# A causal convolution of matrices on one core: one-bank seeds, weights cast while they are loaded, and a start on TensorE

## The chip, the cores and the metric

One core of a Trainium2 chip runs the whole program. The time is the device time of one execution in microseconds (us). The span of a profile is about 2 us shorter than the time, which also holds the launch. TensorE does the matmuls, VectorE and ScalarE the elementwise work, GpSimd issues the DMAs that cast, and SyncE the plain ones and the DMA transposes.

## The reference

```python
B, S, D, K = 8, 4096, 512, 8
out = np.zeros_like(x)                       # x: (B, S, D) fp32, kernel: (K, D, D) fp32
for k in range(K):
    shifted = x if k == 0 else np.concatenate(
        [np.zeros((B, k, D), dtype=np.float32), x[:, :-k, :]], axis=1)
    out += np.matmul(shifted, kernel[k])
```

Each output row is a sum of eight row-by-matrix products. The kernel cuts the 32,768 rows into 128 runs of 256 time steps, one run a partition, and takes eight time steps of all runs at once: this is "a step" below, and there are 32. Applying a three-products-for-four scheme three times over, it does 27 products a step instead of 64. The price is sums: of weights once, of x in each step, and of partial results.

## The kernel before

A step has three nodes (MID, LO, HI) of nine products. A product is four matmuls of 128 x 128 x 512. A node begins with a "seed": a shared partial sum in two banks of PSUM (512 fp32 a bank), from which its two outputs start.

```python
    def node_u(i, a):
        ...
        product(n.q[:, 1], n.s[0], W[a, MID, MID], True)
        nc.scalar.copy(out=n.q[:, 0], in_=n.q[:, 1])          # between banks
    def node_a(n):
        product(n.q[:, 0], n.s[1][0], W[n.a, MID, LO], False)
        product(n.q[:, 1], n.s[1][1], W[n.a, MID, HI], False)
        nc.scalar.copy(out=n.ts, in_=n.q)                     # two banks to SBUF
    def node_v(n, b_):
        product(p[:, 1], n.s[2][b_], W[n.a, b_, MID], True)
        tt(p, p[:, 1:2].to_broadcast([P, 2, D]), n.ts, ADD if b_ == LO else SUB)   # VectorE, two banks
```

Within the node loop the sums of x stand between the nodes' work. D421's upper half, which the HI node multiplies, is summed after the seeds of that node:

```python
        if nxt:
            node_v(nxt, 0)
            node_v(nxt, 1)
        ...
        elif a == LO:
            prep_d421(HI)
```

At the start, x goes through DMA transposes. Then the weights come in four rounds of fp32, each summed in fp32 by VectorE and cast or negated by ScalarE:

```python
        for c in range(DC):                      # 4 rounds, all 27 weights need all 4
            ... nc.sync.dma_start(out=wt, in_=kr[:, c, 4 * h:4 * h + 4, :])
            ... tt(mid4, ...); tt(mid2, ...); tt(W[a, b_, MID][:, c], V[:, 0], V[:, 1], ADD)
            ... nc.scalar.copy(...); nc.scalar.mul(..., mul=-1.0)
```

## Time and profile before

| | kernel before |
|---|---|
| time, median of 3 | 925.17 us (924.97 to 925.95) |
| span of the profiled run | 922.9 us |
| TensorE's first full stretch of matmuls | at 112.21 us, 1 of 864 products done |
| one step | 25.165 us |
| TensorE's own work in a step | 108 x 0.216 = 23.33 us |
| VectorE busy in a step | 23.22 us |
| waits in the even stage | 59.9 us |

The last row: the last matmul ends at 917.71, so the even stage takes 917.71 - 112.21 = 805.5 us. The 863 products left take 863 x 4 x 0.216 = 745.6 us. The rest, 59.9 us, is time in which TensorE waits. Two parts of the time can therefore be cut: the start, and the step's wait. The views that show this stand in the prediction.

### The profile page before, as it was taken

How to read it: one execution, taken by the hardware profiler on the slowest of the kernel's cores; microseconds unless marked ns; L12 is line 12 of the kernel's file. 1: busy time of each engine (PE TensorE's matmuls, PEld its weight loads, DVE VectorE, ACT ScalarE, POOL GpSimd, SP SyncE). 2: the span in 40 equal slices, each digit the busy share in tenths (PEclk: the TensorE clock that was granted, in tenths of full speed). 3: DMA queues.
4: the chain of work that ended last, by engine and by line, in shares of the span. 5: the costliest groups of instructions: out<-in, count | busy, mean ns of one | idle time of the engine just before them, and what ended most of it. 6: DMA issues, size and time to landing. Idle time of an engine off the chain costs nothing.

```text
span 922.9 us, 9305 instructions
## 1 busy us (share of the span) xinstructions
PE 758.2 (82%) x3464; PEld 336.7 (36%) x3464; DVE 793.2 (86%) x954; ACT 255.9 (28%) x329; POOL 43.0 (5%) x86
## 2 busy tenths in 40 slices
PE   1000199999999999999999999999999999999997
PEld 0000044444444444444444444444444444444443
DVE  0358679999999999999999999999999999999996
ACT  0046622222222222222222222222222222222222
POOL 4000000000000000000000000000000000000000
PEclk9999999999999999999999999999999999999999
DMA  7853317867787767677776676767677876676642
GB/s 95 116 202 130 91 40 165 181 153 174 178 173 172 158 163 179 153 161 165 182 173 157 173 180 166 155 166 177 143 172 165 181 167 166 171 182 165 155 136 114
DMA packets 169709, 145.25 MB, mean 157 GB/s; under 512 B 140752, under 2 KB 140752, under 8 KB 169664
## 3 DMA queue, kind: packets, MB, share of 16 engines
q1 hardware_dynamic: 159936, 110.12, 44.0%
q0 software_dynamic: 9728, 34.54, 23.7%
q8 instruction: 27, 0.44, 0.2%
q14 instruction: 18, 0.15, 0.1%
HBM read 77.46 MB, written 67.11 MB: 157 GB/s over the span
## 4 chain that ended last, share of the span: by engine, by line
PE 61%; DVE 21%; issue 5%; ACT 0%; DVEq 0%
PE pp L181 61%; DVE D L79 11%; DVE pp L79 7%; DVE y L79 4%; ACT ts L209 0%; DVEq L79 0%; ACT w L172 0%; ACT pp L202 0%
## 5 line engine op out<-in xcount | busy, mean ns | idle before, releaser
L181 PE MATMUL pp<-w,D 128*128 128x512 bf16 x3328 | 730.5, 380 | 61.9 <-DVE D L79 53.2
L181 PEld LDWEIGHTS <-D 128*128 128x128 bf16 x3328 | 323.2, 98 | 479.0 <-DVE D L79 69.0
L79 DVE TENSOR_TENSOR pp<-pp,ts 128x1024 f32<-128x1024 f32 x192 | 226.5, 1225 | 26.2 <-ACT ts L209 26.2
L79 DVE TENSOR_TENSOR D<-D 128x512 bf16<-128x512 bf16 (+3 forms) x353 | 239.5, 731 | 0.0
L79 DVE TENSOR_TENSOR y<-pp,ms 128x1024 f32<-128x1024 f32 x128 | 156.3, 1221 | 46.4 <-PE pp L181 46.4
L79 DVE TENSOR_TENSOR D<-XT 128x512 bf16<-128x512 bf16 (+3 forms) x226 | 152.5, 722 | 34.0 <-DMA XT<-xin 34.0
L209 ACT COPY ts<-pp 128x1024 f32<-128x1024 f32 x96 | 97.2, 1013 | 276.3 <-PE pp L181 272.8
L202 ACT COPY pp<-pp 128x512 f32<-128x512 f32 x96 | 54.7, 570 | 236.4 <-PE pp L181 236.4
L181 PE MATMUL pp<-w,XT 128*128 128x512 bf16 x128 | 34.2, 385 | 96.2 <-DVE w L79 96.2
L226 ACT COPY ms<-pp 128x1024 f32<-128x1024 f32 x64 | 64.9, 1014 | 69.5 <-PE pp L181 69.5
L91 POOL DMA_DIRECT2D xin<-in_x_dram x64 | 34.0, 531 | 827.9 <-DMA XT<-xin 827.9
L181 PEld LDWEIGHTS <-XT 128*128 128x128 bf16 x128 | 12.5, 98 | 98.5 <-issue 83.8
L79 DVE TENSOR_TENSOR mid<-wt 128x1024 f32<-128x1024 f32 (+1 forms) x12 | 18.9, 1576 | 17.2 <-DMA wt<-in_kernel_dram 17.2
L171 ACT CAST w<-mid 128x512 bf16<-128x512 f32 x20 | 12.1, 605 | 71.8 <-DVE mid L79 71.8
L79 DVE TENSOR_TENSOR w<-mid 128x512 bf16<-128x512 f32 x20 | 13.1, 689 | 0.4
L172 ACT ACTIVATE w<-mid 128x512 bf16<-128x512 f32 x20 | 12.5, 625 | 0.0
L79 DVE TENSOR_TENSOR w<-wt 128x512 bf16<-128x512 f32 x16 | 10.3, 684 | 0.0
L172 ACT ACTIVATE w<-wt 128x512 bf16<-128x512 f32 x16 | 10.0, 625 | 0.0
L171 ACT CAST w<-wt 128x512 bf16<-128x512 f32 x16 | 9.6, 602 | 0.0
L95 POOL DMA_DIRECT2D xin<-in_x_dram x16 | 8.3, 530 | 1.2 <-DVE xin L93 1.2
L79 DVE TENSOR_TENSOR mid<-mid 128x1024 f32<-128x1024 f32 x4 | 4.9, 1225 | 0.3
L85 PE MATMUL pp<-zero,ident 128*128 128x512 bf16 x8 | 3.6, 630 | 1.4 <-POOL ident masks.py:199 1.4
(10 smaller groups left out, 5.3 us busy)
## 6 DMA issues: line engine op xcount, KB each, us to landing
out_dram<-y SPq DMA_DIRECT2D x128, 512.0 KB, 3.0
xin<-in_x_dram POOLq DMA_DIRECT2D x64, 512.0 KB, 5.4
wt<-in_kernel_dram SPq DMA_DIRECT2D x8, 1024.0 KB, 4.8
XT<-xin SPq DMA_TRANSPOSE x66, 5.0
xin<-in_x_dram POOLq DMA_DIRECT2D x16, 60.0 KB, 2.6
```

The lines of the kernel that those rows point to most:

```text
L79: nc.vector.tensor_tensor(out=o, in0=a, in1=b, op=op)
L85: nc.tensor.matmul(pw[:, h], lhsT=ident, rhs=zero, start=True, stop=True)
L91: nc.gpsimd.dma_start(out=xin, in_=xr[:, K * i + 4 * h:K * i + 4 * h + 4, :])
L95: nc.gpsimd.dma_start(out=xin[b * G + 1:(b + 1) * G], in_=xr[b * G:(b + 1) * G - 1, RUN - 8 + 4 * h:RUN - 4 + 4 * h, :])
L171: nc.scalar.copy(out=W[a, b_, LO][:, c], in_=V[:, 1])
L172: nc.scalar.mul(out=W[a, b_, HI][:, c], in_=V[:, 0], mul=-1.0)
L181: nc.tensor.matmul(bank, lhsT=comp[:, c * P:(c + 1) * P], rhs=w[:, c, :], start=start and c == 0, stop=c == DC - 1, skip_group_check=True)
L202: nc.scalar.copy(out=n.q[:, 0], in_=n.q[:, 1])
L209: nc.scalar.copy(out=n.ts, in_=n.q)
L226: nc.scalar.copy(out=ms[b_], in_=p)
```

## The change

Its intent is to halve VectorE's work on seeds, to put D421 ahead of them, and to begin multiplying as soon as the first weights are there. The core of the diff:

```diff
+    def node_a1(i, a):
+        product(n.q[:, 1], n.s[1][1], W[a, MID, HI], True)
         nc.scalar.copy(out=n.q[:, 0], in_=n.q[:, 1])
+    def node_a0u(n):
         product(n.q[:, 0], n.s[1][0], W[n.a, MID, LO], False)
-        product(n.q[:, 1], n.s[1][1], W[n.a, MID, HI], False)
-        n.ts = cpool.tile([P, 2, D], f32, name="ts")
-        nc.scalar.copy(out=n.ts, in_=n.q)
+        product(n.q[:, 1], n.s[0], W[n.a, MID, MID], False)
+    def node_seed(n):                            # ScalarE puts the seed into one bank of each pair
+        for b_ in range(2):
+            n.p[b_] = ppool.tile([P, 2, D], f32, name="pp")
+            ... nc.scalar.copy / nc.scalar.mul(-1.0) (out=n.p[b_][:, 1], in_=n.q[:, 1])
+        nc.scalar.copy(out=n.dts, in_=n.q[:, 0])
     def node_v(n, b_):
-        product(p[:, 1], n.s[2][b_], W[n.a, b_, MID], True)
-        tt(p, p[:, 1:2].to_broadcast([P, 2, D]), n.ts, ADD if b_ == LO else SUB)
+        product(p[:, 1], n.s[2][b_], W[n.a, b_, MID], False)
+        ... tt(p[:, 0], n.dts, p[:, 1], SUB)     # VectorE: one bank (or scalar_tensor_tensor)
... sums of x merged, with row steps of -7, -3, -6:
-        tt(D1[:, 0], XT[:, 7], XT[:, 0], SUB)
-        tt(D1[:, 1], XT[:, 0], XT[:, 1], SUB)
+        tt(D1[:, 0:2], XT[:, 7::-7], XT[:, 0:2], ADD)
... the start: each tap one DMA that casts fp32 to bf16; mids summed as bf16
+    def load_w(tap):
+        n = K - 1 - tap
+        nc.gpsimd.dma_start(out=W[n >> 2, n >> 1 & 1, n & 1], in_=kr[:, :, tap, :])
+    for tap in (6, 4, 7, 5): load_w(tap)         # weights of the LO node first
+    xi.append(load_x(0, 1))
+    for tap in (2, 0, 3, 1): load_w(tap)
+        transpose_pe(T, xi[0], range(0, 4))      # TensorE transposes the first step's x
+        transpose_pe(H, D421, range(0, 8))       # and the rows before it
... order of nodes and of TensorE's products
-    order = [(i, a) for i in range(NIT) for a in (MID, LO, HI)]
+    order = [(0, LO), (0, HI), (0, MID)]
+    order += [(i, a) for i in range(1, NIT) for a in (MID, LO, HI)]
         if nxt:
-            node_a(nxt)
+            node_a0u(nxt)
+        if k >= 2:
+            node_l(cur, 1, LO)                   # one product between the seed and its use
+        ... node_seed(nxt); ... prep_d421(HI); ... node_v(nxt, 0); node_v(nxt, 1)
```

More of the change, by code (lines that the diff above doesn't have):

```diff
@@ L53 @@
     xpool = ctx.enter_context(tc.tile_pool(name="x", bufs=2))
-    ppool = ctx.enter_context(tc.tile_pool(name="p", bufs=4, space=PSUM))
     ctx.enter_context(tc.manual_schedule())
@@ L63 @@
     W = {}
-    for a in (MID, LO, HI):
-        for b_ in (MID, LO, HI):
-            for c_ in (MID, LO, HI):
+    for a in (LO, HI, MID):
+        for b_ in (LO, HI, MID):
+            for c_ in (LO, HI, MID):
                 W[a, b_, c_] = wpool.tile([P, DC, D], bf, name=f"w{a}{b_}{c_}")
@@ L76 @@
     D1 = spool.tile([P, 2, D], bf, name="D1")
+    F2 = spool.tile([P, 5, D], bf, name="F2")
+    F21 = spool.tile([P, 4, D], bf, name="F21")
+    F1 = spool.tile([P, 2, D], bf, name="F1")
+    F0 = spool.tile([P, D], bf, name="F0")
     def tt(o, a, b, op):
         nc.vector.tensor_tensor(out=o, in0=a, in1=b, op=op)
-    for _ in range(4):
-        pw = ppool.tile([P, 2, D], f32, name="pp")
-        for h in range(2):
-            nc.tensor.matmul(pw[:, h], lhsT=ident, rhs=zero, start=True, stop=True)
     def load_x(i, h):
         xin = xpool.tile([P, 4, D], bf, name="xin")
-        if i >= 0:
-            nc.gpsimd.dma_start(out=xin, in_=xr[:, K * i + 4 * h:K * i + 4 * h + 4, :])
-        else:
-            nc.vector.memset(xin, 0.0)
-            for b in range(B):
-                nc.gpsimd.dma_start(
-                    out=xin[b * G + 1:(b + 1) * G],
-                    in_=xr[b * G:(b + 1) * G - 1, RUN - 8 + 4 * h:RUN - 4 + 4 * h, :])
+        nc.gpsimd.dma_start(out=xin, in_=xr[:, K * i + 4 * h:K * i + 4 * h + 4, :])
         return xin
@@ L103, in transpose_x, with pairs @@
             in_=xin.rearrange("p j d -> p (j d)"))
+    def pairs(z):
+        return z.rearrange("p (a b) d -> p a (b d)", b=2)
     def prep_m():
-        tt(D1[:, 0], XT[:, 7], XT[:, 0], SUB)
-        tt(D1[:, 1], XT[:, 0], XT[:, 1], SUB)
-        tt(D2[:, 0:2], XT[:, 6:8], XT[:, 0:2], ADD)
-        tt(D2[:, 2:4], XT[:, 0:2], XT[:, 2:4], ADD)
+        tt(D1[:, 0:2], XT[:, 7::-7], XT[:, 0:2], ADD)
+        tt(pairs(D2[:, 1:5]), pairs(XT)[:, 3::-3], pairs(XT)[:, 0:2], ADD)
     def prep_d27():
-        tt(D2[:, 4], XT[:, 5], XT[:, 7], ADD)
+        tt(D2[:, 0], XT[:, 5], XT[:, 7], ADD)
     def prep_d21():
-        tt(D21[:, 0], D2[:, 4], D2[:, 0], SUB)
-        tt(D21[:, 1:4], D2[:, 0:3], D2[:, 1:4], SUB)
+        tt(D21[:, 0:4], D2[:, 0:4], D2[:, 1:5], ADD)
     def prep_d4(h):
@@ L121, in prep_d4, with prep_d41, prep_d42 @@
         tt(D4[:, 4 * h:4 * h + 4], a, b, ADD)
-    def prep_d41_d42(h):
+    def prep_d41(h):
         if h == LO:
-            tt(D41[:, 0], D4[:, 7], D4[:, 0], SUB)
-            tt(D41[:, 1], D4[:, 0], D4[:, 1], SUB)
-            tt(D42[:, 0:2], D4[:, 6:8], D4[:, 0:2], ADD)
-            tt(D42[:, 2:4], D4[:, 0:2], D4[:, 2:4], ADD)
-        else:
-            tt(D41[:, 2:4], D4[:, 3:5], D4[:, 4:6], SUB)
+            tt(D41[:, 0:2], D4[:, 7::-7], D4[:, 0:2], ADD)
+        else:
+            tt(D41[:, 2:4], D4[:, 3:5], D4[:, 4:6], ADD)
+    def prep_d42(h):
+        if h == LO:
+            tt(pairs(D42)[:, 0:2], pairs(D4)[:, 3::-3], pairs(D4)[:, 0:2], ADD)
+        else:
             tt(D42[:, 4:8], D4[:, 2:6], D4[:, 4:8], ADD)
@@ L134, in prep_d421 @@
         if h == LO:
-            tt(D421[:, 0], D42[:, 7], D42[:, 0], SUB)
-            tt(D421[:, 1:4], D42[:, 0:3], D42[:, 1:4], SUB)
-        else:
-            tt(D421[:, 4:8], D42[:, 3:7], D42[:, 4:8], SUB)
-    xi = [load_x(-1, 0), load_x(-1, 1)]
-    for h in range(2):
-        transpose_x(xi[h], h)
-    tt(D4[:, 5:8], XT[:, 1:4], XT[:, 5:8], ADD)
-    tt(D42[:, 7], D4[:, 5], D4[:, 7], ADD)
-    tt(D2[:, 4], XT[:, 5], XT[:, 7], ADD)
-    xi = [load_x(0, 0), load_x(0, 1)]
-    transpose_x(xi[0], 0)
@@ L149 @@
-    prep_m()
-    prep_d4(LO)
-    prep_d21()
-    prep_d41_d42(LO)
-    transpose_x(xi[1], 1)
-    prep_d4(HI)
-    xi = [load_x(1, 0), load_x(1, 1)]
-    with tc.tile_pool(name="wt", bufs=1) as tp:
-        for c in range(DC):
-            halves = []
-            for h in range(2):
-                wt = tp.tile([P, 4, D], f32, name="wt", bufs=3)
-                nc.sync.dma_start(out=wt, in_=kr[:, c, 4 * h:4 * h + 4, :])
-                halves.append(wt)
-            mid4 = tp.tile([P, 4, D], f32, name="mid4")
-            tt(mid4, halves[0], halves[1], SUB)
-            for a, A in ((MID, mid4), (LO, halves[1]), (HI, halves[0])):
-                mid2 = tp.tile([P, 2, D], f32, name="mid2", bufs=2)
-                tt(mid2, A[:, 0:2], A[:, 2:4], SUB)
-                for b_, V in ((MID, mid2), (LO, A[:, 2:4]), (HI, A[:, 0:2])):
-                    tt(W[a, b_, MID][:, c], V[:, 0], V[:, 1], ADD)
-                    nc.scalar.copy(out=W[a, b_, LO][:, c], in_=V[:, 1])
-                    nc.scalar.mul(out=W[a, b_, HI][:, c], in_=V[:, 0], mul=-1.0)
@@ L174 @@
-    mpool = ctx.enter_context(tc.tile_pool(name="m", bufs=3))
+            tt(D421[:, 0:4:2], D42[:, 7:0:-6], D42[:, 0:4:2], ADD)
+            tt(D421[:, 1:4:2], D42[:, 0:4:2], D42[:, 1:4:2], ADD)
+        else:
+            tt(D421[:, 4:8], D42[:, 3:7], D42[:, 4:8], ADD)
+    nc.vector.memset(D421, 0.0)
+    xi = [load_x(0, 0)]
+    for b in range(B):
+        nc.gpsimd.dma_start(out=D421[b * G + 1:(b + 1) * G, 1:8],
+                            in_=xr[b * G:(b + 1) * G - 1, RUN - 7:RUN, :])
+    def load_w(tap):
+        n = K - 1 - tap
+        nc.gpsimd.dma_start(out=W[n >> 2, n >> 1 & 1, n & 1], in_=kr[:, :, tap, :])
@@ new lines, in mid_a, with mid_b, mid_c, transpose_pe @@
+    def mid_a(b_, c_):
+        tt(W[MID, b_, c_], W[HI, b_, c_], W[LO, b_, c_], SUB)
+    def mid_b(a, c_):
+        tt(W[a, MID, c_], W[a, HI, c_], W[a, LO, c_], SUB)
+    def mid_c(a, b_):
+        tt(W[a, b_, MID], W[a, b_, LO], W[a, b_, HI], SUB)
+    for tap in (6, 4, 7, 5):
+        load_w(tap)
+    xi.append(load_x(0, 1))
+    for tap in (2, 0, 3, 1):
+        load_w(tap)
+    with tc.tile_pool(name="t", bufs=1, space=PSUM) as tpool:
+        H = tpool.tile([P, K, D], bf, name="hist")
+        T = tpool.tile([P, K, D], bf, name="xt0")
+        def transpose_pe(o, src, ts_):
+            for t in ts_:
+                for c in range(DC):
+                    nc.tensor.transpose(o[:, t, c * P:(c + 1) * P],
+                                        src[:, t % src.shape[1], c * P:(c + 1) * P], ident)
+        transpose_pe(T, xi[0], range(0, 4))
+        transpose_pe(H, D421, range(0, 8))
+        nc.scalar.copy(out=XT[:, 0:4], in_=T[:, 0:4])
+        nc.scalar.copy(out=F0, in_=T[:, 0])
+        hs = D421[:, 4:8]
+        nc.scalar.copy(out=hs, in_=H[:, 4:8])
+        tt(D4[:, 5:8], H[:, 1:4], hs[:, 1:4], ADD)
+        tt(D4[:, 0:4], hs, XT[:, 0:4], ADD)
+        prep_d41(LO)
+        mid_b(LO, HI)
+        tt(D42[:, 7], D4[:, 5], D4[:, 7], ADD)
+        prep_d42(LO)
+        mid_c(LO, LO)
+        prep_d421(LO)
+        mid_b(LO, LO)
+        mid_c(LO, MID)
+        mid_c(LO, HI)
+        transpose_pe(T, xi[1], range(4, 8))
+        nc.scalar.copy(out=XT[:, 4:8], in_=T[:, 4:8])
+        tt(F1[:, 0], hs[:, 3], XT[:, 0], ADD)
+        tt(F1[:, 1], XT[:, 0], XT[:, 1], ADD)
+        tt(F2[:, 0], hs[:, 1], hs[:, 3], ADD)
+        tt(F2[:, 1:3], hs[:, 2:4], XT[:, 0:2], ADD)
+        tt(F2[:, 3:5], XT[:, 0:2], XT[:, 2:4], ADD)
+        tt(F21, F2[:, 0:4], F2[:, 1:5], ADD)
+        prep_d4(HI)
+        prep_d41(HI)
+        prep_d42(HI)
+        prep_d421(HI)
+        prep_d27()
@@ L175 @@
+    xi = [load_x(1, 0), load_x(1, 1)]
+    ppool = ctx.enter_context(tc.tile_pool(name="p", bufs=3, space=PSUM))
+    qpool = ctx.enter_context(tc.tile_pool(name="q", bufs=1, space=PSUM))
+    for k in range(4):
+        pw = ppool.tile([P, 2, D], f32, name="pp") if k else qpool.tile([P, 2, D], f32, name="qq")
+        for h in range(2):
+            nc.tensor.matmul(pw[:, h], lhsT=ident, rhs=zero, start=True, stop=True)
+    mpool = ctx.enter_context(tc.tile_pool(name="m", bufs=2))
     cpool = ctx.enter_context(tc.tile_pool(name="c", bufs=2))
@@ L186, with streams @@
         pass
-    def streams(a):
+    def streams(i, a):
+        if a == MID and i == 0:
+            return (F0, [F1[:, 0], F1[:, 1]], [F2[:, 1], F2[:, 3]],
+                    [F21[:, j] for j in range(4)])
         if a == MID:
-            return (XT[:, 0], [D1[:, 0], D1[:, 1]], [D2[:, 0], D2[:, 2]],
+            return (XT[:, 0], [D1[:, 0], D1[:, 1]], [D2[:, 1], D2[:, 3]],
                     [D21[:, j] for j in range(4)])
@@ L195, in streams @@
                 [D421[:, o + j] for j in range(4)])
-    def node_u(i, a):
+    def node_a1(i, a):
         n = Node()
-        n.i, n.a, n.s = i, a, streams(a)
-        n.q = ppool.tile([P, 2, D], f32, name="pp")
-        product(n.q[:, 1], n.s[0], W[a, MID, MID], True)
+        n.i, n.a, n.s = i, a, streams(i, a)
+        n.q = qpool.tile([P, 2, D], f32, name="qq")
+        product(n.q[:, 1], n.s[1][1], W[a, MID, HI], True)
         nc.scalar.copy(out=n.q[:, 0], in_=n.q[:, 1])
+        n.p = {}
         return n
-    def node_a(n):
+    def node_a0u(n):
         product(n.q[:, 0], n.s[1][0], W[n.a, MID, LO], False)
-        product(n.q[:, 1], n.s[1][1], W[n.a, MID, HI], False)
-        n.ts = cpool.tile([P, 2, D], f32, name="ts")
-        nc.scalar.copy(out=n.ts, in_=n.q)
-        n.p = {}
-    def node_v(n, b_):
-        n.p[b_] = p = ppool.tile([P, 2, D], f32, name="pp")
-        product(p[:, 1], n.s[2][b_], W[n.a, b_, MID], True)
-        tt(p, p[:, 1:2].to_broadcast([P, 2, D]), n.ts, ADD if b_ == LO else SUB)
+        product(n.q[:, 1], n.s[0], W[n.a, MID, MID], False)
+    def node_seed(n):
+        for b_ in range(2):
+            n.p[b_] = ppool.tile([P, 2, D], f32, name="pp")
+            if b_ == LO:
+                nc.scalar.copy(out=n.p[b_][:, 1], in_=n.q[:, 1])
+            else:
+                nc.scalar.mul(out=n.p[b_][:, 1], in_=n.q[:, 1], mul=-1.0)
+        n.dts = cpool.tile([P, D], f32, name="dts")
+        nc.scalar.copy(out=n.dts, in_=n.q[:, 0])
+    def node_v(n, b_):
+        p = n.p[b_]
+        product(p[:, 1], n.s[2][b_], W[n.a, b_, MID], False)
+        if b_ == LO:
+            tt(p[:, 0], n.dts, p[:, 1], SUB)
+        else:
+            nc.vector.scalar_tensor_tensor(out=p[:, 0], in0=p[:, 1], scalar=-1.0,
+                                           in1=n.dts, op0=MUL, op1=SUB)
     ms = {}
@@ L220, in node_l, with store @@
         product(n.p[b_][:, j], n.s[3][2 * b_ + j], W[n.a, b_, j], False)
+    def store(i, a, b_, y):
+        t0 = K * i + 4 * a + 2 * b_
+        nc.sync.dma_start(out=orr[:, t0:t0 + 2, :], in_=y)
+    first = {}
     def node_e(n, b_):
         p = n.p[b_]
-        if n.a == MID:
+        if n.i == 0 and n.a == MID:
+            for a in (LO, HI):
+                y = first[a, b_]
+                tt(y, y, p, ADD if a == LO else SUB)
+                store(0, a, b_, y)
+        elif n.a == MID:
             ms[b_] = mpool.tile([P, 2, D], f32, name="ms")
@@ L228, in node_e @@
             y = ypool.tile([P, 2, D], f32, name="y")
-            tt(y, p, ms[b_], ADD if n.a == LO else SUB)
-            t0 = K * n.i + 4 * n.a + 2 * b_
-            nc.sync.dma_start(out=orr[:, t0:t0 + 2, :], in_=y)
-    order = [(i, a) for i in range(NIT) for a in (MID, LO, HI)]
-    nodes = [node_u(*order[0])]
-    node_a(nodes[0])
+            if n.i == 0:
+                nc.scalar.copy(out=y, in_=p)
+                first[n.a, b_] = y
+            else:
+                tt(y, p, ms[b_], ADD if n.a == LO else SUB)
+                store(n.i, n.a, b_, y)
+    order = [(0, LO), (0, HI), (0, MID)]
+    order += [(i, a) for i in range(1, NIT) for a in (MID, LO, HI)]
+    nodes = [node_a1(*order[0])]
+    node_a0u(nodes[0])
+    node_seed(nodes[0])
     node_v(nodes[0], 0)
     node_v(nodes[0], 1)
-    nodes.append(node_u(*order[1]))
     for k, (i, a) in enumerate(order):
         cur = nodes[k]
-        nxt = nodes[k + 1] if k + 1 < len(order) else None
-        last = i + 1 == NIT
-        if a == MID and not last:
+        stage = k % 3
+        more = i + 1 < NIT
+        if stage == 0 and more:
             transpose_x(xi[0], 0)
@@ L246 @@
         node_l(cur, 0, HI)
-        node_e(cur, 0)
-        if nxt:
-            node_a(nxt)
-        if a == MID:
-            prep_d421(LO)
-        elif not last and a == LO:
-            prep_m()
-            prep_d4(LO)
-        elif not last:
+        if k < 2:
+            node_l(cur, 1, LO)
+            node_l(cur, 1, HI)
+            node_e(cur, 0)
+            if k == 0:
+                mid_b(HI, HI)
+                mid_c(HI, LO)
+                mid_b(HI, LO)
+                mid_c(HI, MID)
+                mid_c(HI, HI)
+                nodes.append(node_a1(*order[1]))
+            else:
+                mid_a(LO, HI)
+                mid_a(HI, HI)
+                mid_b(MID, HI)
+                mid_a(LO, LO)
+                mid_a(HI, LO)
+                mid_b(MID, LO)
+                mid_c(MID, MID)
+                mid_c(MID, LO)
+                mid_c(MID, HI)
+                nodes.append(node_a1(*order[2]))
+            node_e(cur, 1)
+        nxt = nodes[k + 1] if k + 1 < len(order) else None
+        if nxt:
+            node_a0u(nxt)
+        if k >= 2:
+            node_l(cur, 1, LO)
+            node_e(cur, 0)
+        if nxt:
+            node_seed(nxt)
+        if stage == 0:
+            if i:
+                prep_d421(LO)
+                prep_d41(HI)
+        elif stage == 1:
+            if more:
+                prep_m()
+            if i:
+                prep_d421(HI)
+        elif more:
+            prep_d41(LO)
+            prep_d42(LO)
             prep_d21()
-            prep_d41_d42(LO)
         if nxt:
@@ L260 @@
             node_v(nxt, 1)
-        if a == MID:
-            prep_d41_d42(HI)
-            prep_d27()
-        elif a == LO:
-            prep_d421(HI)
-        elif not last:
-            prep_d4(HI)
-        node_l(cur, 1, LO)
-        if k + 2 < len(order):
-            nodes.append(node_u(*order[k + 2]))
-        node_l(cur, 1, HI)
-        node_e(cur, 1)
-        if a == LO and not last:
+        if stage == 0:
+            if i:
+                prep_d42(HI)
+                prep_d27()
+        elif more:
+            prep_d4(LO if stage == 1 else HI)
+        if k >= 2:
+            node_l(cur, 1, HI)
+        if 1 <= k and k + 2 < len(order):
+            nodes.append(node_a1(*order[k + 2]))
+        if k >= 2:
+            node_e(cur, 1)
+        if stage == 1 and more:
             transpose_x(xi[1], 1)
```

## The prediction

> **What bounds the kernel now.** I read the page first, for the shares, then the windows of the start and of three single steps, then the waits, then the timeline of one step, and last the groups by form for the price of each kind of instruction.
>
> ```profile
> span 922.9 us, 9305 instructions
> PE 758.2 (82%) x3464; PEld 336.7 (36%) x3464; DVE 793.2 (86%) x954; ACT 255.9 (28%) x329; POOL 43.0 (5%) x86
> PE   1000199999999999999999999999999999999997
> PEclk9999999999999999999999999999999999999999
> ```
>
> The shares name no winner: VectorE 86%, TensorE 82%. But the slices show two kernels: a start in which TensorE does nothing, then one even stage at full clock. So I take them apart.
>
> ```profile
> 0.00:112.00 112.00, 5.93 (x12) 1.49 (x13) 57.11 (x70) 39.47 (x74) 11.74 (x27) 1.00 0.59 129
> 311.53:336.69 25.16, 23.48 (x108) 10.50 (x109) 23.22 (x29) 6.78 (x8) 1.06 (x2) 1.00 0.70 167
> 336.69:361.86 25.17, 23.49 (x109) 10.51 (x109) 23.22 (x29) 6.78 (x8) 1.06 (x2) 1.00 0.73 168
> 361.86:387.02 25.16, 23.48 (x108) 10.46 (x109) 23.22 (x29) 6.78 (x8) 1.06 (x2) 1.00 0.71 167
> ```
>
> The columns are PE, PEld, DVE, ACT, POOL busy with instruction counts, then clock and DMA. A step (8 time steps of every run, 27 products of 4 matmuls) takes 25.165 us, 32 of them. Neither engine fills it. What is missing is one wait:
>
> ```profile
> PE pp L181 <- DVE w L79: 96.2, 4, 53.6
> PE pp L181 <- DVE D L79: 53.2, 32, 1.7
> ```
>
> The first line is the start (TensorE waits for combined weights), the second is once a step: 53.2 / 32 = 1.66 us. The timeline shows which instruction ends it:
>
> ```profile
> 311.53 21.76 PE L181 MATMUL pp<-w,D 128*128 128x512 bf16 x100 [1.68 <-DVE D L79]
> 330.15 3.09 DVE L79 TENSOR_TENSOR D<-XT 128x512 bf16<-128x512 bf16 x5
> 333.12 1.03 PE L181 MATMUL pp<-w,XT 128*128 128x512 bf16 x4
> 333.15 2.36 DVE L79 TENSOR_TENSOR pp<-pp,ts 128x1024 f32<-128x1024 f32 x2
> 334.24 0.57 ACT L202 COPY pp<-pp 128x512 f32<-128x512 f32 x1 [2.49 <-PE pp L181]
> 335.42 1.22 DVE L79 TENSOR_TENSOR D<-D 128x2048 bf16<-128x2048 bf16 x1
> ```
>
> VectorE makes five sums of x, then the two seeds of a node (1.2 us each), and only then D421's upper half (ends 336.64), which TensorE's next product needs; it resumes at 336.69. VectorE is late, in order, on a step in which it is busy 23.2 us. TensorE's own floor: 100 matmuls in 21.76 us, the last one lasting 0.38, so (21.76 - 0.38) / 99 = 0.2160, and over 80 in 17.45 (chain of waits) 0.2161; I use 0.216. 108 x 0.216 = 23.33 us. So a step holds 25.165 - 23.33 = 1.84 us that is not matmul: the 1.68 us wait plus the 0.16 us by which the last matmul before it outlasts its pitch.
>
> **What the Trainium skill says.** "TensorE: Matmul & The Clock Gate", section "Wait - 56ns, not 53.3ns?", gives 215.7 ns from start to start of warm 512-column matmuls and 426.7 cold. The trace agrees: 0.216 in the step, and about 0.43 for the first matmuls after an idle start (weight loads at 112.59, 113.02, 113.44). So 23.3 us is a floor for a step.
>
> "VectorE: DVE Perf Modes", section "The perf-mode tier table", has tensor_tensor run two elements a cycle for bf16 in SBUF and one for any PSUM operand. The trace agrees:
>
> ```profile
> L79 DVE TENSOR_TENSOR pp<-pp,ts 128x1024 f32<-128x1024 f32 x139 | 164.0, 1225 | 11.7 <-ACT ts L209 11.7
> L79 DVE TENSOR_TENSOR y<-pp,ms 128x1024 f32<-128x1024 f32 x92 | 112.3, 1221 | 33.0 <-PE pp L181 33.0
> L79 DVE TENSOR_TENSOR D<-D 128x2048 bf16<-128x2048 bf16 x46 | 55.9, 1216 | 0.0
> L79 DVE TENSOR_TENSOR D<-D 128x1024 bf16<-128x1024 bf16 x69 | 45.3, 683 | 0.0
> L79 DVE TENSOR_TENSOR D<-D 128x512 bf16<-128x512 bf16 x92 | 36.4, 416 | 0.0
> ```
>
> 1024 fp32 from PSUM cost as much as 2048 bf16. "Vector Engine (DVE) Microarchitecture Reference", section 5.1, lists operands with a negative step among what is not measured; the change uses them, and no run here shows them yet. "DMA: Bandwidth & Descriptors", section "SWDGE vs HWDGE vs iDMA", ties a cast during DMA to the GpSimd queue. The x loads of before are such casts, so their rate is a measured stand-in for the weights.
>
> **The change, part by part.** (1) One-bank seeds. Before, a node's VectorE work is two 1024-wide fp32 sums; after, ScalarE copies the seed into one bank of each pair and VectorE makes only the other: two of 512. The y rows have 1221 for 1024; by the skill's one element a cycle (0.96 GHz) half as many save 0.53, so 0.69 us. Six a step: 7.35 falls to 4.14.
> (2) The bf16 sums of a step merge from 18 instructions to 13: seven of 2048, five of 1024, one of 512: 7 x 1.216 + 5 x 0.684 + 0.417 = 12.35 us. Before: 4 x 1.216 + 5 x 0.684 + 2 x 0.951 + 7 x 0.417 = 13.1.
> (3) y stays, 4 x 1.221 = 4.88. VectorE's sum is 12.35 + 4.14 + 4.88 = 21.4 against 25.3. Consecutive instructions overlap by about 0.08 (a 2048 sum started at 310.26, the next at 311.39: 1.13 for 1.21); before, 25.3 shows as 23.2 busy. After: some 19.8 to 20.1.
> (4) ScalarE: per node the copy between banks, two seeds and one fp32 half, 4 x 0.57 = 2.28, plus two ms copies a step: 3 x 2.28 + 2 x 1.01 = 8.9 us, from 6.8. Far from a bound.
> (5) Order: D421's upper half now goes ahead of the node's seed sums. I laid one node (9 products, 7.78 us) on a time line. In the two heavy nodes VectorE starts y at 1.97 us (product 2 ends 1.73, plus 0.16 tail, plus 0.09 to the start), does y and three sums by 6.0, the seed halves by 7.3, D4 by 8.4, y by 9.5, i.e. 1.8 us into the next node, just in time; in the light node it rests 2 us. TensorE needs the first seed half at 7.78 and has it at 6.7. So the 1.84 us go.
> (6) A new round trip comes: the product after the seeds needs ScalarE's copy. From the trace the copy starts 0.09 us after the end of the product (333.12 + 1.03 = 334.15, copy at 334.24), lasts 0.57, and TensorE resumes 0.06 after (112.15 to 112.21). The last matmul of the seed product starts at s and ends at s + 0.38, so the seed is there at s + 1.10. The change puts one other product in between, so the slot is s + 5 x 0.216 = s + 1.08. A stall of 0.02 to 0.03 a node: 95 nodes, 2.4 us in all.
>
> **The start.** Before, the first full stretch of matmuls begins at 112.21, and only one product of the 864 is done by then.
>
> ```profile
> 68.96 2.29 DVE L79 TENSOR_TENSOR mid<-wt 128x2048 f32<-128x2048 f32 x1 [3.19 <-DMA wt<-in_kernel_dram]
> 111.58 0.57 ACT L202 COPY pp<-pp 128x512 f32<-128x512 f32 x1
> 112.21 19.77 PE L181 MATMUL pp<-w,D 128*128 128x512 bf16 x84 [8.67 <-ACT pp L202]
> q0 software_dynamic: 9728, 34.54, 23.7%
> ```
>
> The weights come in four rounds of 14.8 us (54.16, 68.96, ...) after 43.6 us of DMA transposes. After, everything comes on the GpSimd queue as bf16. Its rate by the last line: 34.54 MB / (0.237 x 922.9 us) = 158 GB/s. Up to the second half of x lie 0.52 + 0.86 + 4 x 0.52 + 0.52 = 4.0 MB: 25 us, plus 4 for first issue and landing: 29 to 30. TensorE, in order, may not pass its transposes: 16 x 0.11 = 2, the ScalarE copy of 2048 (1.9, from 0.57 for 512 and 1.01 for 1024), 8 warm-up matmuls at 0.43 = 3.4: the first node starts near 37.5. A node alone is 9 x 0.864 plus 0.9 for each of its two ScalarE trips and some 0.2: 9.75. First node to 47.2, second to 57 (its last weight lands near 43, so it doesn't wait). The third needs nine sums of weights on VectorE, which start after the second node's seeds, about 54.2: nine at 1.13 plus self-waits, 64.8; then two sums of x, 66.5, its first seed half, 67.2. There the steady stage starts, with 23 products done and 841 left: 841 x 0.864 = 726.6. Sum: 67 + 727 + 2.4 + tail 5.2 (last matmul ended at 917.7 of 922.9) + 2.3 (925.17 less the span) = 804; I take a us off for sums that overlap: 803 us. Against 925 the saving splits into some 58 us of steps (1.84 x 31.5) and some 65 of the start (112 to 67, and 22 products at 0.864 more done by then), less the new trips.
>
> **The rivals.** Negative row steps lose the two-a-cycle rate: five of the merged sums slow down, three of 1024 by 0.53 and two of 2048 by 1.07: 3.7 us a step, VectorE at 23.8, above TensorE's 23.3, with waits a step of 24.3 and a total near 834. For: the skill calls it unmeasured. Against: inside a row all is dense, with step 1. Second, the seed trip is longer than one product: each 0.1 us more per node costs 9.5 us, 812. Against: the latencies above are of the same copy in the same place. Third, the starting loads are slower, as their rows are shorter (1 KB written a packet, 4 KB for x) and eight are of 15 partitions: at 110 GB/s the first node starts 11 us later, 814; at 180, 3 us earlier. Fourth, the DMA transpose of x now starts later in its step: it lands 5.5 us after issue (313.07 to the buffer's release at 318.61), near 7.7 us of the node in which VectorE wants it at 7.2. The light node after it absorbs this; if not, 0.5 us a step, 818.
>
> **Range and chances.** The rivals of the start move the time by -4 to +11, those of the step by 0 to +30, of which I hold 0 to +10 likely. So 790 to 822 eight times in ten. Even with the worst two together it stays under 850, 8% less; faster by over 2% 0.98, within 2% 0.015, slower 0.005.
>
> **What would show it.** Steps of 23.3 to 23.5 us, the wait for D gone, VectorE busy about 20 of them, seed halves at 0.69, merged sums at 1.22 and 0.68; TensorE waiting on ScalarE under 5 us in the steady stage; the steady stage from about 67 us. It would be wrong with steps over 24 us, or with the steady stage starting past 80 us.

## The result, and the profile after

The changed kernel takes **795.83 us** (median of 4 runs, 795.29 to 796.77), against 925.07 (923.69 to 925.95) for the kernel before in the same rounds. The ratio is 0.8605, with an interval of 0.859 to 0.862. The result is correct.

The head of the page of the changed kernel, with the row of TensorE's busy tenths in 40 slices:

```profile
span 793.6 us, 9335 instructions
PE 760.0 (96%) x3528; PEld 345.7 (44%) x3528; DVE 662.3 (83%) x762; ACT 277.6 (35%) x455; POOL 44.7 (6%) x86
PE   2579999999999999999999999999999999999997
```

TensorE is at 96%, and the empty slices at the left are gone. The window of one step, from the start of one product to the start of the same product a step later (columns as in the prediction):

```profile
311.41:334.73 23.32, 23.32 (x109) 10.54 (x108) 19.88 (x24) 8.38 (x14) 1.06 (x2) 1.00 0.76 171
```

A step now takes 23.32 us and TensorE is busy in all of it: it runs at its own floor. VectorE has 3.4 us to spare. Two of the seven kinds of wait that TensorE has in the whole run (total, times, longest):

```profile
PE xt L167 <- DMA xin<-in_x_dram: 15.4, 2, 8.6
PE qq L217 <- DVE w L82: 3.4, 3, 2.5
```

The wait for D, once a step before, is in none of the seven lines; all seven lie in the start. The timeline of one step shows both reasons, the place of D421 and the seed's trip:

```profile
316.21 1.22 DVE L82 TENSOR_TENSOR D<-D 128x2048 bf16<-128x2048 bf16 x1
317.35 0.69 DVE L82 TENSOR_TENSOR pp<-dts,pp 128x512 f32<-128x512 f32 x1
321.78 1.03 PE L217 MATMUL qq<-w,XT 128*128 128x512 bf16 x4
322.65 3.62 PE L217 MATMUL pp<-w,D 128*128 128x512 bf16 x16
322.85 0.57 ACT L259 COPY pp<-qq 128x512 f32<-128x512 f32 x1 [2.83 <-PE qq L217]
```

The sum of 2048 that makes D421's upper half is done at 317.43, ahead of the seed sums, which are 0.69 us each now. TensorE ends the seed product at 321.78 + 1.03 = 322.81; ScalarE's copy starts 0.04 later and ends at 323.42. The product that covers it occupies TensorE from 322.65 for 4 x 0.216, to 323.51. The margin is under 0.1 us, but it is one: TensorE's line runs on with no wait. In one node of three, though, the margin is gone. There the copy starts 0.09 us after its product, at 315.12 for 313.14 + 1.89 = 315.03:

```profile
313.14 1.89 PE L217 MATMUL qq<-w,D 128*128 128x512 bf16 x8
315.12 0.57 ACT L259 COPY pp<-qq 128x512 f32<-128x512 f32 x1 [1.95 <-PE qq L217]
```

The starts of single matmuls in the trace show that TensorE then goes on 0.013 us late, in 30 nodes, 0.4 us in all. Why this copy starts later than the other two isn't shown.

The start and the last matmuls, from the timeline:

```profile
25.05 1.89 PE L167 MATMUL xt<-ident,xin 128*128 128x128 bf16 x16 [8.57 <-DMA xin<-in_x_dram]
32.25 1.91 PE L217 MATMUL qq<-w,D 128*128 128x512 bf16 x4
49.56 10.67 DVE L82 TENSOR_TENSOR w<-w,w 128x2048 bf16<-128x2048 bf16 x9
56.76 1.04 PE L217 MATMUL qq<-w,F 128*128 128x512 bf16 x4 [2.49 <-DVE w L82]
62.63 1.89 PE L217 MATMUL pp<-w,F 128*128 128x512 bf16 x8 [0.18 <-DVE pp L82]
781.57 7.08 PE L217 MATMUL pp<-w,D 128*128 128x512 bf16 x32
```

The second half of x lands at 25.0, the first node begins at 32.25 and the second at 42.75. The nine sums of weights for the third run from 49.56, and TensorE waits for them. The even stage begins at 62.63 us with 24 products done, and the last matmul ends at 781.57 + 7.08 = 788.65.

**Where 129.3 us of span went** (922.9 less 793.6). The even stage starts 112.21 - 62.63 = 49.6 us earlier, and 23 more products are done by then, worth 23 x 0.864 = 19.9 us: the start gives 69.5. From 62.63 to the last matmul's end at 788.65 are 726.0 us, and 840 products need 840 x 0.864 = 725.8: 0.2 us of waits by this rounded pitch, where there were 59.9. So the steps give 59.7. The tail is 0.2 us shorter (5.19 to 4.95). The sum is 129.4, equal within rounding.

### The profile page after: what moved, and what is told of

It is laid out like the page before. It is cut to its first block, busy times and chain, and to the rows that moved or that the text cites. A ratio compares the mean times of both kernels' runs of the same rounds, so it can differ in the third digit from the quotient of the medians. Undisturbed runs are those within 1.5% of the kernel's fastest.

```text
span 793.6 us, 9335 instructions
## 1 busy us (share of the span) xinstructions
PE 760.0 (96%) x3528; PEld 345.7 (44%) x3528; DVE 662.3 (83%) x762; ACT 277.6 (35%) x455; POOL 44.7 (6%) x86
## 3 DMA queue, kind: packets, MB, share of 16 engines
q0 software_dynamic: 13696, 38.61, 30.4%
## 4 chain that ended last, share of the span: by engine, by line
PE 94%; DMA 2%; DVE 2%; ACT 1%; issue 0%; POOL 0%; ACTq 0%
PE pp L217 62%; PE qq L217 31%; DMA xin<-in_x_dram 2%; DVE w L82 1%; DMA D<-in_x_dram 1%; POOL w L143 0%; PE pp L208 0%; PE xt L167 0%; ACT XT L188 0%; DVE D L135 0%; ACT pp L259 0%; DVE y L82 0%; ACT qq L247 0%; PE qq L208 0%; DVE pp L271 0%
## 5 line engine op out<-in xcount | busy, mean ns | idle before, releaser
L217 PE MATMUL pp<-w,D 128*128 128x512 bf16 x2280 | 523.4, 379 | 1.4 <-ACT pp L259 1.3
L217 PE MATMUL qq<-w,D 128*128 128x512 bf16 x1016 | 251.2, 380 | 1.4 <-ACT qq L247 1.4
L82 DVE TENSOR_TENSOR D<-D 128x1024 bf16<-128x1024 bf16 (+1 forms) x256 | 232.0, 947 | 0.1
L82 DVE TENSOR_TENSOR D<-XT 128x2048 bf16<-128x2048 bf16 (+2 forms) x157 | 146.6, 950 | 7.6 <-DMA XT<-xin 6.3
L247 ACT COPY qq<-qq 128x512 f32<-128x512 f32 x96 | 54.7, 570 | 267.3 <-PE qq L217 267.3
L259 ACT COPY pp<-qq 128x512 f32<-128x512 f32 x96 | 54.7, 570 | 177.1 <-PE qq L217 172.7
L82 DVE TENSOR_TENSOR pp<-dts,pp 128x512 f32<-128x512 f32 x96 | 66.4, 692 | 51.5 <-ACT dts L263 47.2
L271 DVE SCALAR_TENSOR_TENSOR pp<-pp,dts 128x512 f32<-128x512 f32 x96 | 66.8, 695 | 3.6
L263 ACT COPY dts<-qq 128x512 f32<-128x512 f32 x96 | 58.2, 606 | 0.0
L261 ACT ACTIVATE pp<-qq 128x512 f32<-128x512 f32 x96 | 56.6, 590 | 0.1
L82 DVE TENSOR_TENSOR w<-w,w 128x2048 bf16<-128x2048 bf16 x19 | 22.4, 1219 | 0.2
## 6 DMA issues: line engine op xcount, KB each, us to landing
w<-in_kernel_dram POOLq DMA_DIRECT2D x8, 512.0 KB, 13.9
```

The costliest lines, as they stand in the source:

```text
L82: nc.vector.tensor_tensor(out=o, in0=a, in1=b, op=op)
L217: nc.tensor.matmul(bank, lhsT=comp[:, c * P:(c + 1) * P], rhs=w[:, c, :], start=start and c == 0, stop=c == DC - 1, skip_group_check=True)
L259: nc.scalar.copy(out=n.p[b_][:, 1], in_=n.q[:, 1])
L261: nc.scalar.mul(out=n.p[b_][:, 1], in_=n.q[:, 1], mul=-1.0)
L263: nc.scalar.copy(out=n.dts, in_=n.q[:, 0])
L271: nc.vector.scalar_tensor_tensor(out=p[:, 0], in0=p[:, 1], scalar=-1.0, in1=n.dts, op0=MUL, op1=SUB)
```

## The experiments

All are the changed kernel with one edit, except where said. They ran on several chips, each beside the kernel before, so I compare with what the changed kernel's ratio makes of that call's time before. In the first two calls (before 922.92 and 923.13) this is 0.8605 x 923 = 794 us.

**1. Two-bank seeds again.** Three ScalarE copies become one, VectorE's seed sums become 1024 wide, order and merged sums stay. Two signs no longer fit. Its output is wrong, which doesn't matter for the time.

```diff
     def node_seed(n):
-        ... (three ScalarE instructions)
+        n.ts = cpool.tile([P, 2, D], f32, name="ts")     # cpool: bufs=1 in place of 2
+        nc.scalar.copy(out=n.ts, in_=n.q)
     def node_v(n, b_):
-        product(p[:, 1], n.s[2][b_], W[n.a, b_, MID], False)
-        ... (one bank)
+        product(p[:, 1], n.s[2][b_], W[n.a, b_, MID], True)
+        tt(p, p[:, 1:2].to_broadcast([P, 2, D]), n.ts, ADD if b_ == LO else SUB)
```

> The changed kernel with the seeds of before: one ScalarE copy of both banks, VectorE makes both halves (1024 wide). Wrong result on purpose (the signs of the two halves no longer fit). Theory: the halved seed work is what keeps VectorE out of TensorE's way. VectorE gets 6 x (1.13 - 0.61) = 3.1 us a step back, about 22.9 of 23.3, and falls behind in the two heavy nodes: steps of 23.8 to 24.6 us, 812 to 835 us. Rival: the new order of the sums alone does it: steps of 23.3, 796 us.

Measured: 806.29 us (805.05 to 808.61), ratio 0.8744 (0.8712 to 0.8775), 12 above 794: between the two theories. The even stage starts at 62.61, as in the changed kernel, so the 10.4 us by which the span is longer (804.0) arose in the steps, 0.34 each. The same product in two steps that follow each other, and the wait:

```profile
355.25 1.89 PE L217 MATMUL pp<-w,D 128*128 128x512 bf16 x8
378.77 1.67 PE L217 MATMUL pp<-w,D 128*128 128x512 bf16 x7
PE pp L217 <- DVE pp L82: 6.2, 13, 0.6
```

A step takes 378.77 - 355.25 = 23.52 us instead of 23.32, and in a stretch of 23.32 us VectorE is busy 22.59. It nearly fits, but it is late with a seed in every step: in most by 0.04 us of idle TensorE, too short for the list of waits, and 0.2 from start to start; the 13 waits of the list are the longer gaps, some of them with a matmul whose record is missing. Wide seeds alone cost about a sixth of the old loss. The edit also leaves one buffer of `ts` in place of two. That is not what costs: 92 of its 96 copies still start 0.04 us after their product.

**2. The sums of x unmerged**, as narrow as before, in their new places and signs.

```diff
-        tt(D1[:, 0:2], XT[:, 7::-7], XT[:, 0:2], ADD)
+        tt(D1[:, 0], XT[:, 7], XT[:, 0], ADD)
+        tt(D1[:, 1], XT[:, 0], XT[:, 1], ADD)
... D2, D21, D41, D42, D421 likewise
```

> The changed kernel with the bf16 sums of x split again as before (18 instructions a step in place of 13). Theory: merging is not what buys the time; VectorE gets some 0.4 us more a step and has room for it: 795 to 798 us, steps 23.3. Rival: the merged sums are needed because the heavy nodes are just in time: a wait of 0.2 us or more in a node, 805 us or more.

Measured: 797.39 us (795.79 to 798.53), ratio 0.864 (0.8615 to 0.8665). It hits. Merging buys TensorE nothing that these runs resolve: VectorE is busy 401.1 instead of 396.7 us in a stretch of 465, work that has room. That is 0.2 us a step. The durations of the sums, added up, differ by 0.7 us a step (13.06 and 12.36); the busy time shows less, as consecutive sums overlap. The profiled run lost some 3 us elsewhere: in the third node, after TensorE's 2.49-us wait for weights, eight matmuls took 3.57 us, where eight take 1.89 in the changed kernel's first profile. They follow each other at 0.427 us, the pace of the first matmuls after an idle start, so I read it as the clock.

**3. D421's upper half after the seeds again**, the seeds staying narrow.

```diff
             if more:
                 prep_m()
-            if i:
-                prep_d421(HI)
...
+            if stage == 1 and i:
+                prep_d421(HI)                    # now after node_v(nxt, 0), node_v(nxt, 1)
```

> The changed kernel with D421's upper half made after the seed halves, as before. Theory: the order counts by itself: the sum ends some 0.4 us after TensorE wants it, one wait a step of 0.3 to 0.5 us, 806 to 812 us. Rival one: the cheaper seeds give enough room, no wait, 796 us. Rival two: the wait comes back whole (1.7 us), 848 us.

Measured: 809.19 us (808.3 to 810.76), ratio 0.8771 (0.8746 to 0.8796), 15 above 794: a hit. The even stage starts at 63.15, so 14.0 us of longer span less 0.5 leave 13.5 for 31 steps, 0.44 each. The old wait is back, once a step:

```profile
PE pp L217 <- DVE D L82: 7.5, 31, 1.1
```

It is 0.24 us of recorded wait, and some 0.2 more by which a matmul before a wait outlasts its pitch. With the rest of the change in place, wide seeds alone cost 10.4 and the late D421 alone 13.5; the kernel before, which has both, loses about 60. My reading is that each of the two nearly fits into the slack that the other leaves, and together they don't. That is argued: no run had both of them in the new order.

**4. No product between the seed and its use.** The new trip to ScalarE is left uncovered.

```diff
+        if k >= 2:
+            node_l(cur, 1, LO)
         if nxt:
             node_a0u(nxt)
         if k >= 2:
-            node_l(cur, 1, LO)
             node_e(cur, 0)
```

> The changed kernel with the covering product moved ahead of the seed's products, so that the seed's first use follows them at once. Theory: the seed's trip through ScalarE (0.1 + 0.57 + 0.06 us after the last matmul's end) is real and hidden by exactly that one product: a wait of 0.8 to 0.9 us in each of 94 nodes, 868 to 882 us. Rival: TensorE had slack anyway or the trip overlaps: under 10 us more, 806 or less.

Measured: 874.16 us (872.95 to 875.42), ratio 0.9473 (0.9445 to 0.9501), 80 above 794: a hit.

```profile
PE pp L217 <- ACT pp L259: 65.3, 95, 1.0
326.14 2.75 PE L217 MATMUL pp<-w,D 128*128 128x512 bf16 x12 [0.66 <-ACT pp L259]
```

The trip costs 80 / 95 = 0.84 us a node when nothing covers it. Without this reordering of TensorE's products the one-bank seeds would have lost more than the whole gain in the steps.

**5. The old start with the new steps.** The start is the kernel before's (fp32 rounds, DMA transposes, MID node first), with signs made to fit the new sums.

```diff
-    (history, taps by casting DMA, TensorE transposes, LO node first)
+    xi = [load_hist(0), load_hist(1)]; transpose_x(...); ...      # as before
+    for c in range(DC): ... tt(mid4, ...) ... nc.scalar.copy ... nc.scalar.mul   # as before
-    order = [(0, LO), (0, HI), (0, MID)]
+    order = [(i, a) for i in range(NIT) for a in (MID, LO, HI)]
```

> The start of before (x and history by DMA transposes, fp32 weight sums in four rounds, node order MID, LO, HI) in front of the new steady stage. Theory: the two halves of the gain add up independently: products start near 112 us, 864 x 0.864 = 746.5, plus 3 for the first node's trips and the cold clock, plus 4.9 and 2.2: 866 to 871 us, so that the steps alone are worth 54 to 59 us and the start 70 to 75. Rival: the new steady stage needs the new start (or the other way round) and the parts do not add: below 860 or above 880.

Measured: 863.28 us (862.35 to 866.03), ratio 0.9354 (0.9324 to 0.9384). Against 794 the start is worth 69 us, and against 923.13 the steps 60, near the 69.5 and 59.7 of the accounting. The match is in part luck. The median lies 3 us under the expected band: the first matmuls after ScalarE's copy of the first seed start at 107.61 here, 4.6 us before that point of the kernel before. I had not foreseen this. The traces show where it comes from: the second DMA transpose took 7.6 us from issue to landing (16.41 to 24.02) instead of 12.9 (16.10 to 28.95), and the weights follow it; why it was faster stays open. So 4.6 of the 60 us belong to this start, and 56.6 of the 61.2 us of span arose after it. On the other side this kernel has 748.9 - 863 x 0.864 = 3.3 us of waits and cold clock after 107.61, where the changed kernel has 0.2 in its even stage; this split counts them to the start.

**6. DMA transposes at the start**, for the first step's x and the rows before it, where the change uses TensorE.

```diff
-        transpose_pe(T, xi[0], range(0, 4))
-        transpose_pe(H, D421, range(0, 8))
+        transpose_x(xi[0], 0)
+        for h in range(2): nc.sync.dma_start_transpose(out=HT[:, 4*h:4*h+4, :]..., in_=D421[:, 4*h:4*h+4, :]...)
... xi[1], the second half of x, likewise
```

> The changed kernel with the first step's x and the history transposed by DMA instead of TensorE. Theory: the four DMA transposes take 5 to 13 us each beside the loads and stand at the head of the VectorE chain of the start: 15 to 25 us later, 811 to 821 us. Rival: the transposes hide behind the weights' arrival: under 4 us, 800 or less.

Measured: 837.38 us (835.08 to 839.35), ratio 0.9067 (0.9037 to 0.9098). The theory had the sign and half of the size: 43 above 794, not about 22. The issue table (last number: median us from issue to landing) and VectorE's first sum:

```profile
HT<-D SPq DMA_TRANSPOSE x2, 26.4
55.62 0.96 DVE L82 TENSOR_TENSOR D<-HT 128x1536 bf16<-128x1536 bf16 x1 [52.34 <-DMA HT<-D]
```

The same first sum starts at 18.41 in the changed kernel. While the cast loads were in flight the two transposes took 23.6 and 29.2 us to land, against a median of 6.2 for those of x in the same run, and the taps, too, took 26.7 instead of 13.9. I had priced the transposes at what they take in a step. Of the parts tried, this is the largest of the start.

**7. The taps as fp32, cast by ScalarE**, over the plain queue with three staging buffers.

```diff
+        staged[tap] = stp.tile([P, DC, D], f32, name="wf")
+        nc.sync.dma_start(out=staged[tap], in_=kr[:, :, tap, :])
-        nc.gpsimd.dma_start(out=W[n >> 2, n >> 1 & 1, n & 1], in_=kr[:, :, tap, :])
+        nc.scalar.copy(out=W[n >> 2, n >> 1 & 1, n & 1], in_=staged[tap])
```

> The changed kernel with the taps loaded as fp32 on the sync queue and cast to bf16 by ScalarE (8 copies of 2048, some 1.9 us each). Theory: the cast by the DMA is a convenience; what counts is that weights are summed as bf16 in 19 instructions and not fp32 in four rounds: 793 to 801 us. Rival: the cast in the DMA itself is worth more than 5 us: 801 or more.

Measured: 812.92 us (812.47 to 813.94), ratio 0.8805 (0.878 to 0.883), 19 above 794. My theory was wrong; the number is where its rival had put it, but the trace gives another reason than the cast's own cost. ScalarE is in order here, so its copy of the transposed x stands behind casts, and a cast stands behind its load:

```profile
34.72 1.90 ACT L151 CAST w<-wf 128x2048 bf16<-128x2048 f32 x1 [4.05 <-DMA wf<-in_kernel_dram]
```

That copy then starts at 36.52; TensorE waits 13.4 us for it and the first node begins at 41.8 instead of 32.25. Three buffers and these places for the casts are one arrangement only. What the cast by the DMA is worth against a better one stays open.

**8. The other four taps first**: those that the LO node doesn't need.

```diff
-    for tap in (6, 4, 7, 5):
+    for tap in (2, 0, 3, 1):
         load_w(tap)
     xi.append(load_x(0, 1))
-    for tap in (2, 0, 3, 1):
+    for tap in (6, 4, 7, 5):
```

> The changed kernel with the HI node's four taps loaded ahead of the LO node's. Theory: the nodes' order fits the order of arrival, and VectorE, in order, waits for the late taps before its sums of x: some 8 us later, 802 to 807 us. Rival: the start is bound by VectorE's and TensorE's work and not by arrival: 796 to 798 us.

Measured: 808.35 us (807.42 to 809.16), ratio 0.8751 (0.8722 to 0.8779), 14 above 794, and just above the expected band. The mechanism holds: VectorE's first sum of weights waits for the late taps.

```profile
31.09 1.23 DVE L82 TENSOR_TENSOR w<-w,w 128x2048 bf16<-128x2048 bf16 x1 [9.90 <-DMA w<-in_kernel_dram]
```

In the changed kernel it starts at 21.14. The even stage starts at 76.31, with the same products done as at 62.63.

**9 to 11. A better start, twice, beside the changed kernel again.** VectorE takes half of ScalarE's copy of the transposed history; six warm-up matmuls go before the second half of x and five after it, where all eight came after it; two of the nine sums of weights move up by one node.

```diff
-        nc.scalar.copy(out=hs, in_=H[:, 4:8])
+        nc.vector.tensor_copy(out=hs[:, 0:2], in_=H[:, 4:6])
+        nc.scalar.copy(out=hs[:, 2:4], in_=H[:, 6:8])
+    (warm-up matmuls here)
         transpose_pe(T2, xi[1], range(0, 4))
...
                 mid_c(HI, HI)
+                mid_a(LO, HI)
+                mid_a(HI, HI)
                 nodes.append(node_a1(*order[1]))
-                mid_a(LO, HI)
-                mid_a(HI, HI)
```

> The changed kernel with a tighter start: the second half of x gets PSUM banks of its own, so that six warm-up matmuls run before it lands; four more keep TensorE busy while ScalarE copies it; VectorE takes half of the history's copy; two of the nine late weight sums move into VectorE's gap before the second node's seed halves. Theory: 2.6 + 0.4 us of warm-up, about 1 of cold clock, 0.9 of copy and 2.3 of weight sums: 788 to 791 us against 796. Rival: one chain on VectorE bounds the start whatever TensorE does: then only the copy and the moved sums count, 792 to 794 us.

Measured: 792.88 us (792.34 to 794.94), ratio 0.8594 (0.8569 to 0.862), too wide to part it from 0.8605, and above the 788 to 791 of the theory. So I ran it with the changed kernel:

> The changed kernel again, unaltered, as the reference of the two runs beside it on the same chip: 794 to 797 us.

> The tighter start once more, beside the changed kernel: its products started 3.6 us earlier in the trace of the first run, so 3 to 4 us less than the changed kernel if that holds in the time, 0 if the difference was the chip's.

Measured (before: 924.82): the changed kernel 797.02 us (796.32 to 797.68), ratio 0.8623 (0.8604 to 0.8643); the better start 792.78 us (792.56 to 793.24), ratio 0.8578 (0.8559 to 0.8597), correct. The ranges of the runs don't touch: 4.2 us, 0.5%, and this version beats both kernels. Its even stage starts at 58.86, against 63.81 for the changed kernel; of these 4.95 us the spans keep 4.0 (790.8 against 794.8), as the tail after the last matmul is 5.9 us instead of 4.9. The point 63.81 is itself 1.2 us later than in the first profile of the changed kernel: x landed 1.3 us later, and after the wait for weights eight matmuls took 3.17 us instead of 2.27. In the better start's profile these matmuls ran warm, so about 1 us of the 4.95 may not be the edit's. TensorE begins its first node 2.5 us earlier (29.79 against 32.25 in the first profile of the changed kernel), and then meets VectorE:

```profile
37.93 3.61 PE L224 MATMUL pp<-w,D 128*128 128x512 bf16 x16 [1.38 <-DVE pp L82]
```

So the number is the rival's, and VectorE's chain of sums bounds the first node now.

**12. That chain on GpSimd.** In the better start the sums for the first step's MID node go to GpSimd.

```diff
-        tt(F1[:, 0], hs[:, 3], XT[:, 0], ADD)
-        ... (6 sums)
+        gg(F1[:, 0], hs[:, 3], XT[:, 0], ADD)    # nc.gpsimd.tensor_tensor
```

> The tighter start with the six sums for the third node moved from VectorE to GpSimd, which is idle then. Theory: VectorE's chain bounds the start, so taking 3.3 us of work out of it brings the steady stage 2 to 3.3 us forward: 2 to 3 us below the tighter start. Rival: GpSimd is slow at it (over 20 us) or keeps VectorE off the memory, so that the third node waits: same or slower than the tighter start.

Measured: 799.2 us (798.67 to 799.44), ratio 0.8646 (0.8627 to 0.8665): 6.4 us worse than without it. VectorE and GpSimd in the timeline:

```profile
28.04 3.14 DVE L82 TENSOR_TENSOR w<-w,w 128x2048 bf16<-128x2048 bf16 x1
30.17 4.91 POOL L86 TENSOR_TENSOR F<-F 128x2048 bf16<-128x2048 bf16 x1
```

The same VectorE sum takes 1.22 us in the changed kernel. The edit also moves the issue of the next step's x; it comes at 19.01 us, against 18.26 in experiment 11, and is no rival. The Trainium skill, "SBUF — State Buffer", section "Who interferes with whom", says that a VectorE instruction with two SBUF inputs contends with a GpSimd instruction that reads SBUF. The trace agrees, at 3.14 against 1.22 us. TensorE then waits 6.08 us in one piece for weights that VectorE sums.

## Why the prediction was right

Predicted were 803 us (790 to 822) and measured 795.83: inside the range, 7 us low. Step by step:

- **The step, right.** Its floor of 23.33 us was measured as 23.32, and the wait for D went. VectorE is busy 19.88 us, inside the predicted 19.8 to 20.1; ScalarE 8.38 instead of 8.9. The saving in the steps was put at 58 us less 2.4 and came to 59.7. The fourth rival, a late DMA transpose of x, fell: in the whole run VectorE waits 6.3 us for x, and TensorE has no wait in the steps. Experiment 3 shows that the order matters, as predicted. But the prediction didn't see how the causes share out: with the rest in place, either narrow seeds or an early D421 already took the larger part.
- **Merging, right in price, without effect.** The prediction's 13.1 and 12.35 us are sums of durations, measured as 13.06 and 12.36. VectorE's busy time falls by only 4.4 us in 465 (experiment 2), and TensorE gains nothing that shows.
- **The rival of the negative row steps fell.** The groups by form, from 310 to 760 us of the changed kernel:

```profile
L82 DVE TENSOR_TENSOR D<-D 128x2048 bf16<-128x2048 bf16 x78 | 93.4, 1218 | 0.0
L82 DVE TENSOR_TENSOR D<-D 128x1024 bf16<-128x1024 bf16 x76 | 48.8, 683 | 0.0
```

  These groups hold three of the five sums with a negative row step, among others, at the 1216 and 683 ns of before; the single durations in the trace are 681 to 684 and 1219 to 1220 ns for all five.
- **The seed trip, mis-sized by 2 us.** The step was a seed ready at s + 1.10 for a slot at s + 1.08, a stall in every node. In two nodes of three the copy starts 0.04 us after the product and not 0.09, so the seed is there at s + 1.05, and the stall is zero. In the third it starts at 0.09 as predicted, and the stall is 0.013 us: 0.4 us in all for a predicted 2.4, and it lies within the 726.0 above. Experiment 4 prices the trip that is hidden here: 0.84 us a node.
- **The start, mis-sized by 4.4 us**: the even stage began at 62.63 and not 67. The term that failed is the landing of x: "29 to 30", from 158 GB/s, was 25.0. In the window from 13 to 25 us the DMA moved 208 GB/s (the last column; the one before is the busy share):

```profile
13.00:25.00 12.00, 3.17 (x28) 2.90 (x28) 6.56 (x8) 1.87 (x1) 2.49 (x4) 1.00 1.20 208
```

  The share is 1.20 of the 16 engines: packets overlap in time. So bytes over the time that packets took is no limit of the rate, and I had used it as one. The third rival, slower loads, erred to the other side. The same quotient for the changed kernel, 38.61 MB over 30.4% of 793.6 us, is again 160 GB/s, while the start ran at 208. From the landing to the first node the trace has 32.25 - 25.0 = 7.25 us for a predicted 7.3; added to 29 to 30 these give 36.3 to 37.3, and 37.5 was written. The first node then took 10.5 us instead of 9.75, as its first matmuls ran at the cold clock (1.91 us for four); by luck this makes up for the 37.5. The second node took its 9.8. The nine sums took 10.67 us for a predicted 10.6, and the later points came about 4.5 us early. (The "43.6 us of DMA transposes" are the point where the loads begin: the transposes run from 9.2 to 43.6, 34.3 us.)
- **The count, one product.** Besides the 23 products I had counted, a further one runs before the even stage, so 840 were left, not 841: 1 us, with rounding.
- **The rest**: the tail was 4.95 for 5.2, the launch 2.2 for 2.3. In the prediction's own sum, where the 726.0 hold what was left of the trips, 4.4 + 1.0 + 2.4 + 0.3 + 0.1 = 8.2 us account for the step from the sum of 804 to 795.8. The one microsecond that I took off for overlap had no term of its own.

What the prediction did not weigh at all is how the start's gain divides. The single undoings cost 43 us (DMA transposes), 19 (this one way of casting on ScalarE) and 14 (order of the taps). They overlap, so they are not to be added; the whole old start, with its order of nodes and its fp32 sums, is 69 (experiment 5).

## What to carry to other kernels

When two engines are both near full, ask in what order the second one reaches what the first needs next, and put that ahead: here an early sum and a halved instruction each removed most of a wait, and it took both to remove all of it. A round trip to another engine can be free when independent work of the first engine lies in it: here one product of 0.86 us hid a trip that costs 0.84 uncovered. So reorder before you add the trip. And price a transfer at a start from a window of the start itself, since neither an average rate of the whole run nor a latency taken from a quiet step holds there.

## What the Trainium skill lacked or had wrong

- "Vector Engine (DVE) Microarchitecture Reference", section 5.1, lists operands with a negative step as not measured. Here, with a negative step between rows and dense rows, the merged bf16 sums took 683 ns for 1024 and 1218 ns for 2048 elements a partition, as without it.
- "SBUF — State Buffer", section "Who interferes with whom", names the contention of VectorE's two-input sums with GpSimd's reads and quotes two slowdowns, but gives no duration for such a sum. In experiment 12 a 2048-wide bf16 sum took 3.14 instead of 1.22 us.
- "TensorE: Matmul & The Clock Gate", section "What's actually happening", has the clock fall after at least one idle window of about 3.4 us, and says that the window is free-running. That passage leaves open what a window with some work in it does. Here a wait of 2.49 us in the third node, with a shorter one before it, could be enough: the next eight matmuls ran cold in experiments 1, 3 and 8 (3.54 to 3.60 us), and warm in the first profile of the changed kernel (four in 1.04).
- No page that I read prices a short trip from TensorE to ScalarE and back: 0.04 or 0.09 us to the copy's start, 0.57 for 512 fp32 between banks, 0.05 to 0.06 to the next matmul; uncovered, 0.84 us a node.
- "DMA: Bandwidth & Descriptors", section "DMA Transpose (X-bar)", has nothing on a DMA transpose beside cast loads: a median of 26.4 us from issue to landing at the start (experiment 6), against 6.2 for the transposes of x in the same run.
